# An RWKV-7 hybrid block on one Trainium2 core: the products of two heads on 64x64 quarters of the array

## The chip, the cores and the metric

The kernel runs on one core of one Trainium2 chip. The metric is the device time of one execution in microseconds (us), as the median of several runs; less is better. The engines are named as the profile names them: PE (TensorE matmul), PEld (TensorE weight load), DVE (VectorE), ACT (ScalarE), POOL (GpSimd) and SP (SyncE, which only issues DMAs here).

## The reference, cut to what matters

One decoder block over 512 tokens of width 2048: a normalised input is projected once, and an RWKV-7 time mixer of 16 heads of 64 and a sliding-window attention run on the result side by side. Gates merge them, and a gated ConvFFN follows. All data are float32. The change lies in the time mixer alone:

```python
def step(state, inp):
    r_t, k_t, v_t, w_t, ka_t, kb_t = inp
    sa = jnp.einsum('bhvk,bhk->bhv', state, ka_t)
    state = (state * w_t[:, :, None, :] + sa[..., None] * kb_t[:, :, None, :]
             + v_t[..., None] * k_t[:, :, None, :])
    y = jnp.einsum('bhvk,bhk->bhv', state, r_t)
    return state, y

state0 = jnp.zeros((B, RW_HEADS, RW_HEAD, RW_HEAD), f32)
_, y = lax.scan(step, state0, xs)
```

So each head has a 64x64 state, and the heads never meet inside the scan.

## The kernel before

The recurrence is computed in 8 chunks of 64 tokens (`NCH` = 8, `C` = 64), and the 16 heads in 8 pairs. A pair fills the 128 partitions: head 0 has the rows 0 to 63 and head 1 the rows 64 to 127 (`HV`). Because one matmul of the full 128x128 array serves both heads, the stationary operands are block diagonal: a 128x128 tile holds one head's 64x64 block in each of two corners and zeros in the others.

For a pair p the code runs `early(p)` (the projections of r, k and v, norms, decays), `late(p)` (the chunk products, the inverse, the chain over the chunks) and `final(p)` (the group norm and the gate). The order of emission is late(p), early(p+1), final(p), then three tiles of the gates' projections. The framework's planner lays out each engine's instructions anew from these, by its own costs, except where the code pins them (`pin`). The projections (`project`, L260 to L262, weights split by ACT in L243 and DVE in L244) are independent of the pairs, and the planner puts them between the matmuls of `late` while those wait for DVE or ACT.

In `late(p)`, with what the change touches:

- `BKK` (L672, L673) holds, for each chunk, the scaled `kb` of a head in the head's own half of the columns and its scaled `k2` in the other half. `BAR` (L674, L675) holds the scaled `kk` and `r`, block diagonal.
- L697 multiplies `BKK` with `BAR`, two chunks to a PSUM tile. L701 masks the result into four tiles: `BX` and `MD` (the kb parts, in the own block, mask "own") and `OA` and `MO` (the k parts, in the other head's block, mask "other"). L702 to L717 and the loop over `LEVELS` (L765 to L790) invert `BX` with f16 products, which the change leaves as they are.
- `VV` (L734) is v with its mean taken off, transposed. Since the k parts lie in the other half, head 0's v goes to the rows of head 1 and the reverse (`ol:oh`).
- `bulk_mm` (L718) runs one 128x128 matmul with 64 moving columns a chunk into one PSUM tile and copies it out with ACT: `GV` = OA x VV, and later `KV` = KO x VV, both through L721.
- `KD` and `KO` (L749, L750) come from transposes of `BKE` (L742): the kb blocks into `KD` in the diagonal corners, the k blocks into `KO` in the off corners. The other corners of `KO` are set to 0 by two POOL memsets (L745, L746) for each pair, as its buffer (tag "ko") serves `OA` and `yd` too.
- The chain over the chunks (L793 to L810): psG (L796, `BAR` x `SS`), added to `GV` by DVE (L798); psU (L802, `BX` x G), copied to `UU` by ACT (L803); psS (L809, `KD` x `UU`), added by DVE (L810) to make the next chunk's state `SS`.
- The output (L815, L816, L818) accumulates three products a chunk in one PSUM tile: `MO` x `VV`, `MD` x `UU`, `BAR` x `SS`.

That is 61 products of 128x128 weights with 64 moving columns for each pair: 8 + 8 (L721), 7 (psG), 8 (psU), 7 (psS), 8 + 8 + 7 (output).

Of the kernel before, what the change touches and what calls it, by code (L numbers as in the profile page):

```python
# [8 lines left out]
F32 = mybir.dt.float32  # L9
# [125 lines left out]
def block_kernel(ctx: ExitStack, tc: tile.TileContext, d: Dims, a: dict, out: bass.AP):  # L135
# [145 lines left out]
    if True:  # L281
# [243 lines left out]
        with ExitStack() as pr:  # L525
# [56 lines left out]
            MO, MD = (bd.tile([P, NCH, P], F32, name=n) for n in ("MO", "MD"))  # L582
# [9 lines left out]
            def r3(ap, c=C):  # L592
                return ap.rearrange("p (n c) -> p n c", c=c)
# [71 lines left out]
            def late(p, st):  # L665
# [27 lines left out]
                OA = wk.tile([P, NCH, P], F32, name="OA", tag="ko")  # L693
                for n0 in range(0, NCH, 2):
                    ps = bulk()
                    for j in range(2):
                        pe.matmul(ps[:, j * 4 * C : (j + 1) * 4 * C], BKK[:, n0 + j],  # L697
                                  BAR[:, n0 + j].rearrange("p a h c -> p (a h c)"), start=True, stop=True)
                    pq = ps.rearrange("p (n a c) -> p n a c", n=2, a=2)
                    for t, a, nm in ((BX, 0, "own"), (OA, 0, "other"), (MD, 1, "own"), (MO, 1, "other")):  # L700
                        dve.tensor_tensor(t[:, n0 : n0 + 2], pq[:, :, a], mb(nm, 2)[:, :, a * P : (a + 1) * P], op=ALU.mult)  # L701
                for g in range(2):  # L702
# [13 lines left out]
                    for i in range(2):  # L716
                        dve.tensor_tensor(BT[:, i, ns], AI[:, i, ns], mb("t1bd", HN), op=ALU.mult)  # L717
                def bulk_mm(dst, l, r):  # L718
                    ps = bulk()
                    for n in range(NCH):  # L720
                        pe.matmul(r3(ps)[:, n], l(n), r(n), start=True, stop=True)  # L721
                    act.activation(dst, r3(ps), AF.Copy)
# [8 lines left out]
                for a, (fl, fh) in enumerate(HV):  # L731
                    for h in range(2):
                        ol, oh = HV[1 - h]
                        dve.tensor_tensor(VV[ol:oh, a::2], r3(ps)[fl:fh, h::2],  # L734
                                          vm[fl:fh, h::2].unsqueeze(2).to_broadcast([C, NT, C]), op=ALU.add)
                GV = wk.tile([P, NCH, C], F32, name="GV", tag="yt")
                bulk_mm(GV, lambda n: OA[:, n], lambda n: VV[:, n])
                for g in range(2):
# [4 lines left out]
                    if g == 0:  # L743
                        KO = wk.tile([P, NCH, P], F32, name="KO", tag="ko")
                        pool.memset(KO[0:C, :, 0:C], 0.0)  # L745
                        pool.memset(KO[C:P, :, C:P], 0.0)  # L746
                    for h, (lo, hi) in enumerate(HV):
                        ol, oh = HV[1 - h]
                        act.activation(KD[lo:hi, ns, lo:hi], ps[lo:hi, :, lo:hi], AF.Copy)  # L749
                        act.activation(KO[lo:hi, ns, ol:oh], ps[lo:hi, :, ol:oh], AF.Copy)  # L750

# [41 lines left out]
                for n in range(NCH):  # L793
                    if n:
                        ps = chn.tile([P, C], F32, name="psG", tag="chn")
                        pe.matmul(ps, BAR[:, n, 0].rearrange("p h c -> p (h c)"), SS[:, n], start=True, stop=True)  # L796
# [5 lines left out]
                    pe.matmul(ps, BX[:, n], G, start=True, stop=True)  # L802
# [6 lines left out]
                    pe.matmul(ps, KD[:, n], UU[:, n], start=True, stop=True)  # L809
# [3 lines left out]
                for n in range(NCH):  # L813
                    dst = r3(ps)[:, n]
                    pe.matmul(dst, MO[:, n], VV[:, n], start=True, stop=False)  # L815
                    pe.matmul(dst, MD[:, n], UU[:, n], start=False, stop=n == 0)  # L816
                    if n:
                        pe.matmul(dst, BAR[:, n, 1].rearrange("p h c -> p (h c)"), SS[:, n], start=False, stop=True)  # L818
# [626 lines left out]
```

## Time and profile before

| what | us |
|---|---|
| median of 3 runs (2877.95 to 2883.97) | 2881.03 |
| the profiled execution's own time | 2880.39 |
| its span | 2878.6 |
| stage of the eight pairs, from the trace | about 330 to 1135 |

A program matmul in float32 shows as two records of PE (and two weight loads of PEld), one in float32r or f16, and a transpose, as one. A row of the timeline has the start, the length, the engine, the line, the operation, what it writes and reads, and how many records in a row it merges; "128*128" is rows by columns of the weights, and the shape behind it that of the moving operand. A record's length is that of its way through the array, so records overlap, and what a matmul costs is read from the distance between the starts. A row of a group has the count, the busy us, the mean ns of one, and the idle time of the engine just before.

### The profile page before, as it was taken

Reading aid. Unit: us, or ns where it says so; the run is one execution under the profiler, and the core shown is the slowest. Engines: PE = TensorE matmul, PEld = TensorE weight load, DVE = VectorE, ACT = ScalarE, POOL = GpSimd, SP = SyncE. Lnnn points to the kernel's source line nnn. Section 1 sums busy time; section 2 is a strip of 40 time slices with the busy share of each in tenths; the row PEclk is TensorE's granted clock in tenths of the full one; section 3 lists DMA queues with packets and bytes.
Section 4 is the critical chain, followed back from the end, with each engine's and each line's share of the span. In section 5 each row is a group of like instructions: output and inputs, shape, how many; then the busy total and the mean of one; then the engine's idle time right before and its main releaser. Section 6 shows DMA issues by size and latency. Waiting matters only on the chain.

```text
span 2878.6 us, 46868 instructions
## 1 busy us (share of the span) xinstructions
PE 2823.6 (98%) x17970; PEld 2476.8 (86%) x17970; DVE 1968.5 (68%) x3388; ACT 1319.8 (46%) x2190; POOL 235.8 (8%) x319
## 2 busy tenths in 40 slices
PE   7999999999999999999999899999999999999999
PEld 6888778878878878788888899999999999888887
DVE  5666677777776775345668787877777787665555
ACT  5345344334434434322456455455555545544444
POOL 0101000000000001011000001101011110000000
PEclk9999999999999999999999999999999999999999
DMA  6865666666656657878777788888888888877775
GB/s 196 227 161 148 184 161 166 155 166 153 165 144 162 169 154 187 269 234 277 255 261 207 211 229 226 224 239 241 227 226 231 239 238 220 316 244 243 257 255 190
DMA packets 223856, 608.35 MB, mean 211 GB/s; under 512 B 24576, under 2 KB 44688, under 8 KB 222608
## 3 DMA queue, kind: packets, MB, share of 16 engines
q1 hardware_dynamic: 156096, 432.86, 45.9%
q0 software_dynamic: 36832, 134.24, 24.3%
q10 hardware_dynamic: 30704, 38.27, 3.9%
q8 instruction: 141, 2.31, 0.3%
q14 instruction: 83, 0.68, 0.1%
HBM read 554.59 MB, written 174.40 MB: 253 GB/s over the span
## 4 chain that ended last, share of the span: by engine, by line
PE 87%; DVE 6%; DMA 3%; issue 1%; ACT 1%; ACTq 0%; SPq 0%; POOL 0%; DVEq 0%; POOLq 0%
PE X L1146 17%; PE X L1013 10%; PE acc L262 9%; PE acc L260 9%; PE acc L261 9%; PE Y L1013 9%; PE Y L1146 8%; PE Z L1146 4%; PE bulk L721 1%; PE bulk L788 1%; PE bulk L758 1%; PE mi L513 1%; PE bulk L606 1%; DMA raw<-in_w_dn_dram 1%; DVE BT L717 1%
## 5 line engine op out<-in xcount | busy, mean ns | idle before, releaser
L260 PE MATMUL acc<-xhi,whi 128*128 128x512 f32 x1120 | 454.1, 405 | 1.8 <-ACT whi L243 1.8
L261 PE MATMUL acc<-xlo,whi 128*128 128x512 f32 x1120 | 454.0, 405 | 0.0
L262 PE MATMUL acc<-xhi,wlo 128*128 128x512 f32 x1120 | 448.6, 401 | 3.2 <-DVE wlo L244 3.2
L243 ACT ACTIVATE whi<-raw 128x512 fp32r<-128x512 f32 x352 | 220.7, 630 | 468.8 <-PE acc L261 364.5
L244 DVE TENSOR_TENSOR wlo<-raw,whi 128x512 fp32r<-128x512 f32 x352 | 240.5, 689 | 231.5 <-ACT whi L243 206.9
L1006 DVE TENSOR_TENSOR wlo<-raw,whi 128x1024 fp32r<-128x1024 f32 x210 | 257.2, 1225 | 204.4 <-ACT whi L1005 204.3
L1005 ACT ACTIVATE whi<-raw 128x1024 fp32r<-128x1024 f32 x210 | 222.6, 1060 | 290.5 <-PE X L1013 155.1
L1146 PE MATMUL X<-b,whi 128*128 128x256 f32 x1472 | 271.0, 284 | 2.5 <-DVE u L1166 0.9
L1146 PE MATMUL X<-t,whi 128*128 128x256 f32 x1408 | 261.2, 286 | 10.1 <-DVE u L1166 9.6
L1129 DVE TENSOR_TENSOR wlo<-raw,whi 128x1024 fp32r<-128x1024 f32 x176 | 215.1, 1223 | 78.7 <-ACT whi L1128 78.3
L1146 PE MATMUL Y<-t,whi 128*128 128x256 f32 x1408 | 257.6, 283 | 0.0
L262 PEld LDWEIGHTS acc<-xhi,wlo 128*128 128x128 f32 x1120 | 212.0, 189 | 45.3 <-DVE wlo L244 7.0
L261 PEld LDWEIGHTS acc<-xlo,whi 128*128 128x128 f32 x1120 | 212.3, 190 | 38.4 <-issue 2.2
L260 PEld LDWEIGHTS acc<-xhi,whi 128*128 128x128 f32 x1120 | 211.8, 189 | 38.7 <-ACT whi L243 2.2
L1128 ACT ACTIVATE whi<-a 128x1024 fp32r<-128x1024 f32 x132 | 139.4, 1056 | 216.2 <-DVE a L1122 212.6
L1146 PEld LDWEIGHTS X<-b,whi 128*128 128x128 f32 x1472 | 231.1, 193 | 3.3 <-issue 2.4
L1146 PEld LDWEIGHTS X<-t,whi 128*128 128x128 f32 x1408 | 222.9, 195 | 10.7 <-DVE u L1166 7.1
L1146 PEld LDWEIGHTS Y<-t,whi 128*128 128x128 f32 x1408 | 220.2, 192 | 0.0
L1146 PE MATMUL X<-b,wlo 128*128 128x256 f32 x736 | 209.5, 285 | 2.1 <-DVE wlo L1129 2.1
L1129 DVE TENSOR_TENSOR wlo<-a,whi 128x1024 fp32r<-128x1024 f32 x132 | 161.7, 1225 | 69.3 <-ACT whi L1128 68.6
L1146 PE MATMUL X<-t,wlo 128*128 128x256 f32 x704 | 200.9, 285 | 0.0
L1146 PE MATMUL Y<-t,wlo 128*128 128x256 f32 x704 | 199.5, 283 | 0.0
(776 smaller groups left out, 6027.2 us busy)
## 6 DMA issues: line engine op xcount, KB each, us to landing
raw<-in_w_up_dram SPq DMA_DIRECT2D x180, 512.0 KB
raw<-in_w_z_dram SPq DMA_DIRECT2D x288, 256.0 KB
s_dn<-in_w_dn_dram POOLq DMA_DIRECT2D x88, 512.0 KB, 7.0
raw<-in_w_up_dram POOLq DMA_DIRECT2D x88, 512.0 KB, 8.6
raw<-s_dn SPq DMA_DIRECT2D x88, 512.0 KB
raw<-in_w_dn_dram SPq DMA_DIRECT2D x66, 512.0 KB
a<-in_w_up_dram SPq DMA_DIRECT2D x48, 512.0 KB
s_dn<-in_w_dn_dram SPq DMA_DIRECT2D x44, 512.0 KB
```

The lines of the kernel that those rows point to most:

```text
L243: pin(act.activation(hi, raw, AF.Copy))
L244: pin(dve.tensor_tensor(lo, raw, hi.bitcast(F32), op=ALU.subtract))
L260: pe.matmul(acc, whi[:, j], xhi[:, k], start=first, stop=False)
L261: pe.matmul(acc, whi[:, j], xlo[:, k], start=False, stop=False)
L262: pe.matmul(acc, wlo[:, j], xhi[:, k], start=False, stop=last)
L513: pe.matmul(ps[:, h], pT[:, kb, h], vt[:, n - 1 + kb, g * HD : (g + 1) * HD], start=kb == kbs[0], stop=kb == kbs[-1])
L1005: act.activation(whi, wr, AF.Copy)
L1006: dve.tensor_tensor(wlo, wr, whi.bitcast(F32), op=ALU.subtract)
L1013: pe.matmul(dst, l[:, q, ts], r[:, es], start=fst and j == 0, stop=lst and j == 2, skip_group_check=True)
L1128: pin(act.activation(hi, t, AF.Copy))
L1129: pin(dve.tensor_tensor(lo, t, hi.bitcast(F32), op=ALU.subtract))
L1146: pin(pe.matmul(ps, l[:, k], r[:, k], start=start and k + i == 0, stop=last and i == 2, skip_group_check=True))
```

## The change

All 61 products are made by head: `heads_mm` runs one matmul on the rows and columns 0 to 63 of the array, then one on 64 to 127, so each uses a 64x64 quarter on the diagonal and reads only its head's block. For that, each head's k parts move into its own rows: `AM` takes the place of `OA` and `MO`, 64 columns wide, written by DVE from the other half's rows of PSUM; `KO` becomes 64 columns wide, written by ACT across the halves, without its memsets; and `VV` stays in its head's own rows. The matmul of L697, the inverse and all transposes stay on the full array.

```diff
--- before.py
+++ after.py
@@ -579,7 +579,8 @@
             BAR = bd.tile([P, NCH, 2, 2, C], F32, name="BAR")
             pool.memset(BAR[0:C, :, :, 1], 0.0)
             pool.memset(BAR[C:P, :, :, 0], 0.0)
-            MO, MD = (bd.tile([P, NCH, P], F32, name=n) for n in ("MO", "MD"))
+            MD = bd.tile([P, NCH, P], F32, name="MD")
+            AM = bd.tile([P, NCH, 2, C], F32, name="AM")
             KD = bdtile("KD")
             SS, UU, VV, KV = (bd.tile([P, NCH, C], F32, name=n) for n in ("SS", "UU", "VV", "KV"))
             Et = bd.tile([P, NCH, C + 1], F32, name="Et")
@@ -690,15 +691,19 @@
 
                 BKE = wk.tile([P, NCH, P], F32, name="BKE", tag="BKE")
                 dve.tensor_tensor(BKE, BKK, ee.unsqueeze(2).to_broadcast([P, NCH, P]), op=ALU.mult)
-                OA = wk.tile([P, NCH, P], F32, name="OA", tag="ko")
                 for n0 in range(0, NCH, 2):
                     ps = bulk()
                     for j in range(2):
                         pe.matmul(ps[:, j * 4 * C : (j + 1) * 4 * C], BKK[:, n0 + j],
                                   BAR[:, n0 + j].rearrange("p a h c -> p (a h c)"), start=True, stop=True)
                     pq = ps.rearrange("p (n a c) -> p n a c", n=2, a=2)
-                    for t, a, nm in ((BX, 0, "own"), (OA, 0, "other"), (MD, 1, "own"), (MO, 1, "other")):
-                        dve.tensor_tensor(t[:, n0 : n0 + 2], pq[:, :, a], mb(nm, 2)[:, :, a * P : (a + 1) * P], op=ALU.mult)
+                    for t, a in ((BX, 0), (MD, 1)):
+                        dve.tensor_tensor(t[:, n0 : n0 + 2], pq[:, :, a], mb("own", 2)[:, :, a * P : (a + 1) * P], op=ALU.mult)
+                    for h, (lo, hi) in enumerate(HV):
+                        rs = slice(*HV[1 - h])
+                        mk = K["other"].rearrange("p (a c) -> p a c", a=2)[rs, :, lo:hi]
+                        dve.tensor_tensor(AM[lo:hi, n0 : n0 + 2], pq[rs, :, :, lo:hi],
+                                          mk.unsqueeze(1).to_broadcast([C, 2, 2, C]), op=ALU.mult)
                 for g in range(2):
                     ns = slice(g * HN, (g + 1) * HN)
                     for h, (lo, hi) in enumerate(HV):
@@ -715,10 +720,15 @@
                     dve.tensor_scalar(BX[C:P, ns, C:P], tt[C:P, ns], 1.0 / SG, None, op0=ALU.mult)
                     for i in range(2):
                         dve.tensor_tensor(BT[:, i, ns], AI[:, i, ns], mb("t1bd", HN), op=ALU.mult)
+                def heads_mm(dst, l, r, start, stop):
+                    for h, (lo, hi) in enumerate(HV):
+                        w = l[lo:hi] if l.shape[-1] == C else l[lo:hi, lo:hi]
+                        pe.matmul(dst[lo:hi], w, r[lo:hi], start=start, stop=stop, skip_group_check=True)
+
                 def bulk_mm(dst, l, r):
                     ps = bulk()
                     for n in range(NCH):
-                        pe.matmul(r3(ps)[:, n], l(n), r(n), start=True, stop=True)
+                        heads_mm(r3(ps)[:, n], l(n), r(n), True, True)
                     act.activation(dst, r3(ps), AF.Copy)
 
                 ps = bulk()
@@ -729,25 +739,22 @@
                 dve.reduce_sum(vm, r3(ps), axis=AX.X)
                 dve.tensor_scalar(vm, vm, -1.0 / HD, None, op0=ALU.mult)
                 for a, (fl, fh) in enumerate(HV):
-                    for h in range(2):
-                        ol, oh = HV[1 - h]
-                        dve.tensor_tensor(VV[ol:oh, a::2], r3(ps)[fl:fh, h::2],
+                    for h, (lo, hi) in enumerate(HV):
+                        dve.tensor_tensor(VV[lo:hi, a::2], r3(ps)[fl:fh, h::2],
                                           vm[fl:fh, h::2].unsqueeze(2).to_broadcast([C, NT, C]), op=ALU.add)
                 GV = wk.tile([P, NCH, C], F32, name="GV", tag="yt")
-                bulk_mm(GV, lambda n: OA[:, n], lambda n: VV[:, n])
+                bulk_mm(GV, lambda n: AM[:, n, 0], lambda n: VV[:, n])
                 for g in range(2):
                     ns = slice(g * HN, (g + 1) * HN)
                     ps = bulk().rearrange("p (n c) -> p n c", c=P)
                     for j in range(HN):
                         pe.transpose(ps[:, j], BKE[:, g * HN + j], ident)
                     if g == 0:
-                        KO = wk.tile([P, NCH, P], F32, name="KO", tag="ko")
-                        pool.memset(KO[0:C, :, 0:C], 0.0)
-                        pool.memset(KO[C:P, :, C:P], 0.0)
+                        KO = wk.tile([P, NCH, C], F32, name="KO", tag="ko")
                     for h, (lo, hi) in enumerate(HV):
                         ol, oh = HV[1 - h]
                         act.activation(KD[lo:hi, ns, lo:hi], ps[lo:hi, :, lo:hi], AF.Copy)
-                        act.activation(KO[lo:hi, ns, ol:oh], ps[lo:hi, :, ol:oh], AF.Copy)
+                        act.activation(KO[ol:oh, ns], ps[lo:hi, :, ol:oh], AF.Copy)
 
                 bulk_mm(KV, lambda n: KO[:, n], lambda n: VV[:, n])
 
@@ -793,29 +800,29 @@
                 for n in range(NCH):
                     if n:
                         ps = chn.tile([P, C], F32, name="psG", tag="chn")
-                        pe.matmul(ps, BAR[:, n, 0].rearrange("p h c -> p (h c)"), SS[:, n], start=True, stop=True)
+                        heads_mm(ps, BAR[:, n, 0].rearrange("p h c -> p (h c)"), SS[:, n], True, True)
                         G = wk.tile([P, C], F32, name="G", tag="G", bufs=2)
                         dve.tensor_tensor(G, GV[:, n], ps, op=ALU.add)
                     else:
                         G = GV[:, 0]
                     ps = chn.tile([P, C], F32, name="psU", tag="chn")
-                    pe.matmul(ps, BX[:, n], G, start=True, stop=True)
+                    heads_mm(ps, BX[:, n], G, True, True)
                     act.activation(UU[:, n], ps, AF.Copy)
                     if n == NCH - 1:
                         break
                     if n:
                         dve.scalar_tensor_tensor(KV[:, n], SS[:, n], ee[:, n : n + 1], KV[:, n], op0=ALU.mult, op1=ALU.add)
                     ps = chn.tile([P, C], F32, name="psS", tag="chn")
-                    pe.matmul(ps, KD[:, n], UU[:, n], start=True, stop=True)
+                    heads_mm(ps, KD[:, n], UU[:, n], True, True)
                     dve.tensor_tensor(SS[:, n + 1], KV[:, n], ps, op=ALU.add)
 
                 ps = bulk()
                 for n in range(NCH):
                     dst = r3(ps)[:, n]
-                    pe.matmul(dst, MO[:, n], VV[:, n], start=True, stop=False)
-                    pe.matmul(dst, MD[:, n], UU[:, n], start=False, stop=n == 0)
+                    heads_mm(dst, AM[:, n, 1], VV[:, n], True, False)
+                    heads_mm(dst, MD[:, n], UU[:, n], False, n == 0)
                     if n:
-                        pe.matmul(dst, BAR[:, n, 1].rearrange("p h c -> p (h c)"), SS[:, n], start=False, stop=True)
+                        heads_mm(dst, BAR[:, n, 1].rearrange("p h c -> p (h c)"), SS[:, n], False, True)
                 yt = wk.tile([P, NCH, C], F32, name="yt", tag="yt")
                 act.activation(yt, r3(ps), AF.Copy)
                 return ag, bon, yt
```

## What the change should do to the time, predicted before it ran

> **What bounds the kernel now.** I read the page first: the busy shares and the chain that ended last. Both name TensorE.
>
> ```profile
> PE 2823.6 (98%) x17970; PEld 2476.8 (86%) x17970; DVE 1968.5 (68%) x3388; ACT 1319.8 (46%) x2190; POOL 235.8 (8%) x319
> PE 87%; DVE 6%; DMA 3%; issue 1%; ACT 1%; ACTq 0%; SPq 0%; POOL 0%; DVEq 0%; POOLq 0%
> ```
>
> A busy matmul row is no proof by itself, since records overlap. So I asked for the stage that the change touches, from the first to the last pair of heads, by the view of windows (length, then busy us of PE, PEld, DVE, ACT, POOL).
>
> ```profile
> 330.00:1135.00 805.00, 795.92 (x5213) 644.38 (x5211) 573.04 (x1377) 343.30 (x748) 63.55 (x86) 1.00 0.63 159
> ```
>
> PE is busy 796 of 805 us at full clock, DVE 573, ACT 343, the DMA engines 63%. The stage holds eight pairs, some 100 us each. What counts is how far apart the matmuls start, which the timeline of PE shows.
>
> ```profile
> 355.99 1.08 PE L721 MATMUL bulk<-VV,KO 128*128 128x64 f32 x8
> 356.90 0.19 PE L758 MATMUL bulk<-XIW,AI 128*128 128x64 f16 x1
> 356.93 0.18 PE L759 MATMUL bulk<-XIW,AI 128*128 128x32 f16 x1
> ...
> 359.04 0.40 PE L260 MATMUL acc<-xhi,whi 128*128 128x512 f32 x1
> ...
> 361.32 0.39 PE L261 MATMUL acc<-xlo,whi 128*128 128x512 f32 x1
> ```
>
> Between 359.04 and 361.32 lie ten projection matmuls, 0.228 us each. The eight records of L721 take 0.91 us, 0.114 each (the other places round to 0.112, which I use). One program matmul in float32 makes two records, so a 128x64 product costs 0.224 us, as much as a projection with eight times the columns. Why 0.112? Look at a record whose weights were already there:
>
> ```profile
> 402.80 0.33 PE L796 MATMUL psG<-SS,BAR 128*128 128x64 f32 x2
> ...
> 403.25 0.40 PE L261 MATMUL acc<-xlo,whi 128*128 128x512 f32 x1
> 403.49 0.39 PE L802 MATMUL psU<-G,BX 128*128 128x64 f32 x2
> 403.69 0.48 PE L262 MATMUL acc<-xhi,wlo 128*128 128x512 f32 x1
> 404.01 0.40 PE L260 MATMUL acc<-xhi,whi 128*128 128x512 f32 x1
> 404.24 0.39 PE L809 MATMUL psS<-UU,KD 128*128 128x64 f32 x2
> 404.46 0.39 PE L816 MATMUL bulk<-UU,MD 128*128 128x64 f32 x2
> 404.69 0.39 PE L818 MATMUL bulk<-SS,BAR 128*128 128x64 f32 x2
> 404.91 0.39 PE L815 MATMUL bulk<-VV,MO 128*128 128x64 f32 x2
> 405.11 0.48 PE L261 MATMUL acc<-xlo,whi 128*128 128x512 f32 x1
> 405.42 0.39 PE L262 MATMUL acc<-xhi,wlo 128*128 128x512 f32 x1
> 405.65 0.33 PE L796 MATMUL psG<-SS,BAR 128*128 128x64 f32 x2
> ...
> L796 PE MATMUL psG<-SS,BAR x112: 217/248/275, 396.2 to 1128.8; 128*128 128x64 f32 x112
> ```
>
> Two psG records together last 0.33, one lasts up to 0.275: the second started 0.055 after the first. So 64 columns stream in 0.055, and the other 0.057 of a usual record is its weight load of 128 columns. These products are bound by weight loads, and half of what is loaded is zeros: the other head's block.
>
> **The change part by part.** How many products? The groups by form, over the stage:
>
> ```profile
> L815 PE MATMUL bulk<-VV,MO 128*128 128x64 f32 x128 | 25.0, 277 | 0.0
> L816 PE MATMUL bulk<-UU,MD 128*128 128x64 f32 x128 | 24.3, 271 | 0.0
> ...
> L818 PE MATMUL bulk<-SS,BAR 128*128 128x64 f32 x112 | 21.6, 275 | 0.0
> L809 PE MATMUL psS<-UU,KD 128*128 128x64 f32 x112 | 21.2, 271 | 0.0
> L802 PE MATMUL psU<-G,BX 128*128 128x64 f32 x112 | 21.0, 270 | 0.6 <-DVE G L798 0.6
> L796 PE MATMUL psG<-SS,BAR 128*128 128x64 f32 x112 | 18.5, 246 | 0.0
> L721 PE MATMUL bulk<-VV,KO 128*128 128x64 f32 x128 | 17.2, 278 | 0.4
> L721 PE MATMUL bulk<-VV,OA 128*128 128x64 f32 x128 | 16.1, 269 | 0.0
> ...
> L802 PE MATMUL psU<-GV,BX 128*128 128x64 f32 x16 | 2.6, 247 | 0.0
> ```
>
> These are 976 records, 488 products, 61 a pair; at 0.112 they hold 109 us of PE. Each becomes two program matmuls of 64x64, four records A1 A2 B1 B2. With half the columns a load takes 0.056, about the 0.055 that a stream takes. No row shows a matmul on fewer than 128 rows, so the price of a pair of heads has two ends. If B's quarter works fully beside A's, it is A's two passes alone: 2 x 0.056 = 0.112. If they go one after the other, 4 x 0.056 = 0.224, what it costs today. In between, B may start a little after A2, and the next A after B2; about the smallest step between two starts in the stage is 0.03 (356.90 to 356.93, L758 to L759). With one such step a product is 0.135 or so, with two 0.166. I take **0.135**: the nearest row is the one that shows load and stream of different matmuls side by side (0.112 for work that one after the other would be 0.167), so the array does run pieces together that don't touch the same weights. It is a choice, not a measurement.
>
> A stretch also pays at its end: the next projection's 128 columns load only after the last pass has begun, 0.112. So a stretch of n products costs (n-1) x 0.135 + 0.139 + 0.112. By stretches, counted in the timeline of 330 to 1135 us, of which the rows above show one chunk of the chain:
>
> - Lone psG and psU between projections, 99: today psU costs 404.01 - 403.25 less two projections, 0.30; after, 0.25. They gain next to nothing; I take 0.
> - psS with the three output products, 48: today 405.42 - 404.01 less two projections, 0.95; after 0.656. 48 x 0.30 = 14 us.
> - L721: a pair has two stretches of four (KO) and one of seven or eight (OA). 16 x (0.91 - 0.57) + 8 x 0.45 = 9 us. The rest, some tens of single products beside other float32 work, 1 us.
>
> That is 24 us of the 109. KO's two memsets go too:
>
> ```profile
> L745 POOL MEMSET KO<- x8: 517/519/519, 354.4 to 1074.0; 64x512 f32 x8
> ...
>   PE bulk L721: 115.1, 7
> ...
>   POOL KO L746: 3.7, 8
> ```
>
> PE's weight loads waited 3.7 us for them in all, partly under a running stream: 0 to 3.7, I take 2. The memset itself stood 115 us in POOL's queue ahead of the adding DMAs of the later stages (L228); these issue earlier, nothing in this stage reads them, so 0 either way. No DMA is added or moved, and no wait: KO's copies still wait for the same transposes, OA's place is taken by AM, which waits like MO for the last output products of the pair before.
>
> On DVE, the masked products of OA and MO become two of 64 rows with as many elements a row:
>
> ```profile
> L701 DVE TENSOR_TENSOR OA<-bulk,cst 128x256 f32<-128x256 f32 x32 | 13.4, 418 | 0.0
> ...
> L734 DVE TENSOR_TENSOR VV<-bulk,vm 64x256 f32<-64x256 f32 x32 | 13.5, 423 | 0.7
> ```
>
> 64 of 0.418 go and 64 of 0.423 (the row that also crosses halves) come: +0.3 us, under PE, as DVE has 232 us free. VV's and KO's copies keep size and number. Without that cover it would be 0.3 us.
>
> Sum: 24 + 2 = 26 us off the profiled execution, which took 2880.39 us (span 2878.6 and 1.8 around it; 0.6 below the median 2881.03): **2854**. With overlap at its best (0.112) the stretches give 36 and the memsets 4, so 2840; with two steps (0.166) 17 and 0, so 2863. [...]
>
> **Changing the shape of the array.** The stretches are entered and left 26 times a pair, 416 changes in all. The trace has one matmul with fewer columns than 128, the transpose of L377:
>
> ```profile
> 396.89 0.39 PE L802 MATMUL psU<-G,BX 128*128 128x64 f32 x2
> 397.01 0.14 PEld L377 LDWEIGHTS bulk<-ident,rq 128*8 128x8 f32 x1
> 397.12 0.27 PE L377 MATMUL bulk<-ident,rq 128*8 128x128 f32 x1
> ...
> 397.23 0.59 PE L628 MATMUL bulk<-thw,wl 128*128 128x512 f32 x1
> ```
>
> psU's two records take 0.23 and L377 0.11 before the next full matmul starts: its stream and nothing more. A load of 8 columns is shorter, too. I cost a change at 0. [...]
>
> **The rivals.** *The heads don't overlap.* All four passes go one after the other at 0.056. For it: no row shows overlap of quarters, and both heads write one PSUM tile. Against: loads and streams do overlap. Lone products gain 0.02, the fours stay at 0.95 (15 x 0.056 + 0.112), so the sum is 0 to -2: 2878 to 2882. [...]
>
> *Changing rows drains the array.* Price: a record of 0.275 has 0.163 left when the next usually starts (0.112 on). With 416 changes that is 68 us, against 26 gained: 2922. It turns slower from 26/416 = 0.063 a change on. For it: no row with fewer rows. Against: L377.
>
> *The chain becomes the bound.* A chunk takes 405.65 - 402.80 = 2.85 us. psG to psU and psU to psS are 0.69 and 0.75 apart, and the two that a DVE or ACT step must fit between lie only two projections apart. The chunk would shrink by 0.3, out of psS to psG (1.41), so the close links stay. If the planned order of PE, which is laid out anew, fits worse, PE idles 0.1 to 0.2 at some of the 22 links a pair: 10 to 26 us given back, 2864 to 2880.
>
> *It doesn't do what it says:* the planner puts projections between A and B. Then lone stretches double and each costs its 0.112: as the first rival or some us worse.
>
> **How the numbers follow.** Forecast with its own range (2840 to 2863): 0.5. Chain gives part back, still faster by over 0.2% (5.8 us, about what a measurement of this kernel can tell): 0.1. No overlap, or all given back, within 0.2%: 0.19. Drains, or doubled stretches: 0.21. The range must reach the no-overlap case and half of the drains (0.1 a change, +15 us): 2838 to 2896. Faster 0.6, same 0.19, slower 0.21.
>
> **What would show it.** In the profile after: records of 64*64; in a stretch of psS and output products, starts of one head's pair 0.056 apart and a product each 0.11 to 0.17 (0.22: no overlap); a projection after a stretch starting no later than today (later by 0.1 or more: drain); lone psG unchanged; KO's memsets gone and OA's products not waiting. The forecast is wrong if product times stay at 0.22, if gaps stand at the borders, or if PE's idle time before psU, psS and psG grows.

## The result, and the profile after

The changed kernel takes 2918.57 us (median of 4 runs, 2915.94 to 2921.25), the kernel before 2880.15 (4 runs, 2877.95 to 2883.97). The ratio is 1.014, with a 95% interval of 1.0122 to 1.0157: 38 us slower. The forecast was 2854, with a range of 2838 to 2896, so both the direction and the range were wrong. A ratio leaves out an execution at a far lower mean clock (one of 3935 us at 0.65 in the first of the kernels with psU alone below, one of 3076 us at 0.85 in the second), while a median counts it.

The profiled execution took 2915.94 us, with a span of 2914.1, 35.5 more than before. The page first, with the same two lines as before:

```profile
PE 2851.2 (98%) x18946; PEld 2443.1 (84%) x18946; DVE 1973.7 (68%) x3388; ACT 1320.3 (45%) x2190; POOL 227.0 (8%) x303
PE 86%; DVE 7%; DMA 3%; ACT 1%; issue 1%; ACTq 0%; SPq 0%; DVEq 0%; POOLq 0%
```

PE has 976 more records, as it should, and is still the bound. DVE's share of the chain has grown from 6 to 7%. All the loss must lie in the pairs' stage. A good ruler for it is the tile `VV`, which DVE writes once a pair: its first and last start lie seven pairs apart. From the view of that tile, before and after (count, ns, first and last start):

```profile
L734 DVE TENSOR_TENSOR VV<-bulk,vm x32: 417/422/429, 350.7 to 1071.5; 64x256 f32<-64x256 f32 x32
```

```profile
L743 DVE TENSOR_TENSOR VV<-bulk,vm x32: 409/422/428, 352.4 to 1111.3; 64x256 f32<-64x256 f32 x32
```

Seven pairs took 720.8 us and take 758.9: **38.1 us**, all of the 35.5 between the two profiled executions and 2.6 more. Every kernel below is read by this ruler, because it leaves out the start, the end and the rest of the program. It is one execution of each, and whole executions of the kernel before differ by up to 6 us.

**What did the products do?** The timeline of PE, one chunk of the chain (four records make one product; the prediction shows the same chunk of before):

```profile
402.94 0.39 PE L260 MATMUL acc<-xhi,whi 128*128 128x512 f32 x1
403.26 0.33 PE L726 MATMUL psU<-G,BX 64*64 64x64 f32 x4
403.53 0.50 PE L261 MATMUL acc<-xlo,whi 128*128 128x512 f32 x1
403.86 0.40 PE L262 MATMUL acc<-xhi,wlo 128*128 128x512 f32 x1
404.19 0.33 PE L726 MATMUL psS<-UU,KD 64*64 64x64 f32 x4
404.36 0.28 PE L726 MATMUL bulk<-UU,MD 64*64 64x64 f32 x4
404.47 0.28 PE L726 MATMUL bulk<-SS,BAR 64*64 64x64 f32 x4
404.59 0.28 PE L726 MATMUL bulk<-VV,AM 64*64 64x64 f32 x4
404.80 0.50 PE L260 MATMUL acc<-xhi,whi 128*128 128x512 f32 x1
405.23 0.33 PE L726 MATMUL psG<-SS,BAR 64*64 64x64 f32 x4
```

Two things stand here. Inside a stretch the products start 404.36 to 404.47 to 404.59, **0.115 us apart**, where the full array needed 0.224: the two heads do run side by side. But every border is late. From the start of a projection to the first product lie 0.32 to 0.33 us (402.94 to 403.26, 403.86 to 404.19), where two projections follow each other at 0.228. The first product of a stretch lasts 0.17 instead of 0.115 (404.19 to 404.36), the last one 0.21 (404.59 to 404.80). The lone psU now costs 403.86 - 402.94 less two projections, 0.46; before it was 0.30.

The weight loads show the border from the other side (timeline of PEld, before and after, at the same psU):

```profile
403.44 0.30 PEld L802 LDWEIGHTS psU<-G,BX 128*128 128x128 f32 x2 [0.23 <-DVE G L798]
...
403.77 0.19 PEld L260 LDWEIGHTS acc<-xhi,whi 128*128 128x128 f32 x1
```

```profile
403.26 0.19 PEld L726 LDWEIGHTS psU<-G,BX 64*64 64x64 f32 x4 [0.37 <-issue]
403.52 0.19 PEld L261 LDWEIGHTS acc<-xlo,whi 128*128 128x128 f32 x1
403.63 0.19 PEld L262 LDWEIGHTS acc<-xhi,wlo 128*128 128x128 f32 x1
```

Before, psU's load began at 403.44, 0.05 ahead of its stream, while a projection ran, and L260's at 403.77, 0.24 ahead of its own. After, the loads of both sides of a border begin with their streams (403.26, and 403.52 for L261 at 403.53); the load unit had stood 0.37 us for nothing that the profile shows. Only L262's load, with no border ahead of it, still comes 0.23 early (403.63 for 403.86). It is the same at the other borders of the seven pairs: loads begin 0.002 us ahead of their streams (the median of 201 entries into a stretch and of 200 exits), against 0.224 between two projections. So in these seven pairs weights aren't loaded ahead across a change of the array's shape.

**What did DVE do?** PE's waits in the stage name it. The view of waits (in total, times, longest), before and after:

```profile
PE acc L262 <- DVE wlo L244: 3.2, 8, 1.2
```

```profile
PE acc L262 <- DVE wlo L244: 10.0, 8, 1.3
```

PE waits 0.85 us longer in each pair for `wlo`, a split of projection weights. The timeline of DVE in the masked products shows why (before, then after; first op, a part, and the op that follows the section):

```profile
437.90 0.42 DVE L701 TENSOR_TENSOR BX<-bulk,cst 128x256 f32<-128x256 f32 x1
438.24 0.42 DVE L701 TENSOR_TENSOR OA<-bulk,cst 128x256 f32<-128x256 f32 x1
...
443.20 0.85 DVE L705 TENSOR_TENSOR tt<-BX,cst 64x256 f32<-64x256 f32 x2
```

```profile
442.61 0.42 DVE L701 TENSOR_TENSOR BX<-bulk,cst 128x256 f32<-128x256 f32 x1
442.95 0.41 DVE L701 TENSOR_TENSOR MD<-bulk,cst 128x256 f32<-128x256 f32 x1
443.38 0.86 DVE L705 TENSOR_TENSOR AM<-bulk,cst 64x256 f32<-64x256 f32 x2
444.26 0.42 DVE L701 TENSOR_TENSOR BX<-bulk,cst 128x256 f32<-128x256 f32 x1
...
449.25 0.85 DVE L710 TENSOR_TENSOR tt<-BX,cst 64x256 f32<-64x256 f32 x2
```

The records are as long as before (0.42), but length isn't the price. Two operations of 128 rows start 0.33 apart, the second before the first has ended. The two of 64 rows take 0.88 from start to start (443.38 to 444.26), 0.44 each, and the `MD` ahead of them takes 0.43 (442.95 to 443.38). The 16 operations took 443.20 - 437.90 = 5.30 us and take 449.25 - 442.61 = 6.64: **1.34 us more a pair**.

**And the clock.** The view of windows has the granted clock (the third number from the right):

```profile
568.60:575.40 6.80, 6.80 (x78) 5.24 (x80) 2.81 (x7) 4.27 (x11) 0.81 (x1) 0.50 0.76 233
677.80:684.60 6.80, 6.80 (x69) 5.24 (x69) 2.97 (x6) 3.95 (x10) 0.81 (x1) 0.50 0.84 247
1002.10:1008.90 6.80, 6.80 (x72) 4.99 (x73) 2.69 (x6) 4.52 (x11) 0.81 (x1) 0.50 0.82 254
```

In three of the seven pairs PE runs at half clock for 6.8 us, soon after its wait for `wlo`; the timeline of PE has the first of these waits:

```profile
566.33 0.50 PE L262 MATMUL acc<-xhi,wlo 128*128 128x512 f32 x1 [1.25 <-DVE wlo L244]
```

The slow stretch begins 2.3 us later, at 568.6, and there are three of them: 3 x 6.8 / 2 = 10.2 us, an estimate from the granted clock of 0.50. Before has no such stretch in its seven pairs (1.00). The records of PE show the loss too: from L262, over 42 records of products, four of L751 and 16 in f16, to the next L260, it took 5.17 us from 568.84 on, and 3.05 for the same records in the pair of 461.83, at full clock; by that share the three cost 8.4. The longest wait for `wlo` was 1.3 us; what sets the drop off was not settled.

So there are three suspects: borders, DVE's 64-row operations, and the clock. A first theory held all three; its rival was that borders alone, or something else in the quarters, made the loss.

### The profile page after: what moved, and what is told of

The parts are those of the page before. It is cut to its first block, busy times and chain, and to the rows that moved or that the text cites. A ratio compares the mean times of both kernels' runs of the same rounds, so it can differ in the third digit from the quotient of the medians.

```text
span 2914.1 us, 48752 instructions
## 1 busy us (share of the span) xinstructions
PE 2851.2 (98%) x18946; PEld 2443.1 (84%) x18946; DVE 1973.7 (68%) x3388; ACT 1320.3 (45%) x2190; POOL 227.0 (8%) x303
## 3 DMA queue, kind: packets, MB, share of 16 engines
q1 hardware_dynamic: 156096, 432.86, 46.5%
## 4 chain that ended last, share of the span: by engine, by line
PE 86%; DVE 7%; DMA 3%; ACT 1%; issue 1%; ACTq 0%; SPq 0%; DVEq 0%; POOLq 0%
PE X L1153 17%; PE X L1020 11%; PE acc L262 9%; PE acc L261 9%; PE acc L260 9%; PE Y L1020 8%; PE Y L1153 8%; PE Z L1153 4%; PE bulk L726 2%; PE bulk L795 1%; PE bulk L765 1%; PE mi L513 1%; DVE AM L705 1%; DVE wlo L244 1%; PE bulk L607 1%
## 5 line engine op out<-in xcount | busy, mean ns | idle before, releaser
L262 PE MATMUL acc<-xhi,wlo 128*128 128x512 f32 x1120 | 449.9, 402 | 10.0 <-DVE wlo L244 10.0
L260 PE MATMUL acc<-xhi,whi 128*128 128x512 f32 x1120 | 456.8, 408 | 2.0 <-ACT whi L243 2.0
L261 PE MATMUL acc<-xlo,whi 128*128 128x512 f32 x1120 | 453.2, 405 | 0.0
L262 PEld LDWEIGHTS acc<-xhi,wlo 128*128 128x128 f32 x1120 | 211.3, 189 | 53.7 <-DVE wlo L244 14.1
L260 PEld LDWEIGHTS acc<-xhi,whi 128*128 128x128 f32 x1120 | 211.4, 189 | 46.0 <-ACT whi L243 2.4
L261 PEld LDWEIGHTS acc<-xlo,whi 128*128 128x128 f32 x1120 | 211.2, 189 | 42.3 <-issue 1.9
```

The lines of the kernel that those rows point to most:

```text
L260: pe.matmul(acc, whi[:, j], xhi[:, k], start=first, stop=False)
L261: pe.matmul(acc, whi[:, j], xlo[:, k], start=False, stop=False)
L262: pe.matmul(acc, wlo[:, j], xhi[:, k], start=False, stop=last)
```

## Experiments

Each is read by the ruler as "seven pairs against before": the last start of `VV` less the first, against 720.8. On the full array a product is 0.224 and on quarters 0.115, so I count 0.109 gained for each.

### The border by itself: psU alone

Three kernels change only psU of the kernel before, 64 of them with a full-array product or projection on each side. The first puts them on quarters:

```diff
-                    pe.matmul(ps, BX[:, n], G, start=True, stop=True)
+                    for lo, hi in HV:
+                        pe.matmul(ps[lo:hi], BX[lo:hi, n, lo:hi], G[lo:hi], start=True, stop=True, skip_group_check=True)
```

> The kernel before, with only the chain's psU (64 products, nearly all alone between full-array matmuls) on two 64x64 quarters; no data moved. Theory 1 (borders: each stretch on quarters costs the array some 0.34 us more at its two ends than on the full array, against 0.109 us gained per product): 64 x (0.34 - 0.11) = +15 us, about 2895. Theory 2 (the moved data and the planner's new order cost the time, the quarters themselves gain): 64 x -0.11 = -7 to 0 us, 2873 to 2880.

The second keeps 128 rows and halves the columns (`BX[:, n, lo:hi], G`):

> The kernel before, with only psU split by columns: two matmuls of 128 rows and 64 columns each, the rows of the other head being zeros. Theory 1a (any change of the array's shape costs, columns as rows): about +15 us, as with quarters. Theory 1b (only a change of rows costs; the transpose with 8 columns showed nothing): between -7 and +1 us, starts at the borders as in the kernel before. Theory 2: as 1b.

The third keeps 128 columns and halves the rows, and leaves out head 1's part of U (`BX[0:C, n], G[0:C]`):

> The kernel before, with psU made of one matmul of 64 rows and 128 columns, head 0's rows alone; head 1's part of U is left out (it becomes zero). A product costs what it did (two records of 128 columns, 0.112 us each), so only the border is left. Theory 1a and 1b: 64 x 0.2 to 0.34 = +13 to +22 us, about 2897. If only narrowed columns cost: 0 us.

Measured: 2890.35 (ratio 1.0029, 1.0011 to 1.0047), 2887.13 (1.0024, 1.0014 to 1.0034) and 2895.91 (1.0058, 1.0041 to 1.0075). The view of the tile `VV` in the first, the second and the third:

```profile
L734 DVE TENSOR_TENSOR VV<-bulk,vm x32: 416/422/429, 353.5 to 1081.9; 64x256 f32<-64x256 f32 x32
```
```profile
L734 DVE TENSOR_TENSOR VV<-bulk,vm x32: 416/422/428, 352.3 to 1080.7; 64x256 f32<-64x256 f32 x32
```
```profile
L734 DVE TENSOR_TENSOR VV<-bulk,vm x32: 416/422/428, 349.2 to 1082.4; 64x256 f32<-64x256 f32 x32
```

Seven pairs take 7.6 us more in the first, as much in the second, and 12.4 in the third, for 56 stretches. In the third, nothing is gained (two records of 128 columns, as before), so 12.4 / 56 = **0.22 us is the bare border, in and out**; it may be more, as the other three executions took 8 us longer than the profiled one. In the first, 7.6 / 56 = 0.14 is left after a gain of 0.109: a border of 0.245. Narrowing the columns alone costs the same as narrowing both, if its product gains as much. So the two changes of a stretch cost 0.22 to 0.25 us in the first and the third. The prediction had costed a change at 0 from the transpose of L377, 128 rows by 8 columns. In the first of these kernels L377 follows psU directly:

```profile
399.92 0.33 PE L803 MATMUL psU<-G,BX 64*64 64x64 f32 x4
400.19 0.27 PE L377 MATMUL bulk<-ident,rq 128*8 128x128 f32 x1
400.30 1.02 PE L628 MATMUL bulk<-thw,wl 128*128 128x512 f32 x2
```

From quarters into L377 is a border (0.27, as into the projection at 403.53 above), and from L377 to the full matmul behind it is none (0.11). Why 8 columns of 128 pass as a full array and 64 don't isn't known.

### The data moved, the products on the full array

The changed kernel with `AM` as two block-diagonal tiles and `heads_mm` as one matmul:

```diff
-                    for h, (lo, hi) in enumerate(HV):
-                        w = l[lo:hi] if l.shape[-1] == C else l[lo:hi, lo:hi]
-                        pe.matmul(dst[lo:hi], w, r[lo:hi], start=start, stop=stop, skip_group_check=True)
+                    pe.matmul(dst, l, r, start=start, stop=stop, skip_group_check=True)
```

> The changed kernel's data in the own head's rows, but every product on the full array: AM as two block diagonal tiles with zero corners, KO written into the first of them, yd in another buffer. DVE has 128 masked products of 64x128 for 64 of 64x256, some 5 us more under PE. Theory 1: as the kernel before, 2875 to 2886. Theory 2 (the move of the data and what the planner makes of it is the loss): 2895 to 2918.

Measured: 2909.33 (1.0108, 1.0093 to 1.0123). This run was meant to isolate the data's part and doesn't: PE stood waiting for `VV`, and that came with seven stretches at half clock, 22 us lost by the trace's record of the clock. By the ruler it takes 34.9 us more. The waits of PE in it:

```profile
PE bulk L725 <- DVE VV L742: 21.0, 7, 3.4
```

That wait isn't in the changed kernel. What the run shows is only how dear a late DVE is here.

### The quarters without the data moved

The kernel before, its data and DVE operations as they were, with GV, KV, psG, psU and psS on quarters (the off-diagonal ones for GV and KV), output products on the full array:

```diff
+                def heads_mm(dst, l, r, other=False):
+                    for h, (lo, hi) in enumerate(HV):
+                        rl, rh = HV[1 - h] if other else (lo, hi)
+                        pe.matmul(dst[lo:hi], l[rl:rh, lo:hi], r[rl:rh], start=True, stop=True, skip_group_check=True)
...
-                        pe.matmul(ps, BAR[:, n, 0].rearrange("p h c -> p (h c)"), SS[:, n], start=True, stop=True)
+                        heads_mm(ps, BAR[:, n, 0].rearrange("p h c -> p (h c)"), SS[:, n])
```

> The kernel before, its data where they were; psG, psU, psS and the GV and KV products on quarters (the k blocks on the two off-diagonal quarters), the output products on the full array. 304 products in 224 stretches. Theory 1 (a stretch costs 0.29 us at its two ends, a product gains 0.109): 65 - 33 = +32 us, about 2911. Theory 2 (the moved data and the plan are the loss, as the run of the layout on the full array suggests): 2846 to 2880.

Measured: 2914.48 (1.0117, 1.0102 to 1.0132), as theory 1 has it. Its `VV`:

```profile
L739 DVE TENSOR_TENSOR VV<-bulk,vm x32: 416/422/428, 350.2 to 1104.0; 64x256 f32<-64x256 f32 x32
```

Seven pairs take 753.8, 33.0 more, with no half-clock stretch and `wlo` waiting 3.2 us as before. Its 266 products in seven pairs gain 29.0, so 196 stretches cost 62, **0.316 each**. That is more than a lone psU showed. A part of it may be what the changed kernel's timeline shows above: a single projection with stretches on both sides pays on entry and exit (404.80 to psG at 405.23 is 0.43 us).

### Longer stretches

Three kernels go from the changed one towards fewer borders. First, psG, psU and psS back on the full array (139 stretches instead of 228). Second, the output products also held in one run behind the last psU (56):

```diff
-                    heads_mm(dst, AM[:, n, 1], VV[:, n], True, False)
-                    heads_mm(dst, MD[:, n], UU[:, n], False, n == 0)
+                    heads_mm(dst, AM[:, n, 1], VV[:, n], True, False, True)
+                    heads_mm(dst, MD[:, n], UU[:, n], False, n == 0, True)
...
```

The last argument pins these matmuls in program order.

Third, GV's products also emitted behind the transposes of `BKE`, in one run with KV's (40):

```diff
-                bulk_mm(GV, lambda n: AM[:, n, 0], lambda n: VV[:, n])
                 for g in range(2):
...
+                bulk_mm(GV, lambda n: AM[:, n, 0], lambda n: VV[:, n])
                 bulk_mm(KV, lambda n: KO[:, n], lambda n: VV[:, n])
```

> The changed kernel with psG, psU and psS back on the full array: 312 products on quarters in 139 stretches. Theory 1: 40 - 34 = +6 us against before, about 2886, and 32 less than the change. Theory 2: the data are still moved, so 2900 to 2918.

> As the run before, and the output products held in program order behind the last psU of the pair, so that they make one stretch: 312 products in 56 stretches. Theory 1: 16 - 34 = -18 us, about 2862. Theory 2: 2900 to 2918.

> As the run before, and GV's products emitted behind the transposes of BKE, in one run with KV's: 312 products in 40 stretches. Theory 1: 12 - 34 = -22 us, about 2857. Theory 2: 2900 to 2918.

Measured: 2897.95 (1.0062, 1.0047 to 1.0077), 2891.62 (1.0045, 1.0029 to 1.0062) and **2867.81 (0.9964, 0.9951 to 0.9977)**. By the ruler they take 19.3 and 14.6 us more than before and 5.5 less. The order is as expected, the sizes aren't: all are 10 us or more above. In the first, PE still waits 9.9 us for `wlo`, and 5.1 us go at half rate. The waits of PE in the second and the third show what stood there:

```profile
PE acc L262 <- DVE wlo L244: 9.9, 8, 1.2
PE bulk L660 <- DVE lw L658: 6.7, 7, 1.0
```

```profile
PE bulk L660 <- DVE lw L658: 6.6, 7, 1.0
PE bulk L726 <- DVE VV L745: 2.5, 7, 0.4
...
PE acc L262 <- DVE wlo L244: 0.5, 1, 0.5
```

In the second, `wlo` waits as in the changed kernel, and the record of the clock has 15 us of the seven pairs lost at half rate; in the third that wait is gone, with GV's run at another place in PE's order, and so are the half-clock stretches in the stage. Both pay a new wait: with the outputs at the end of a pair, the next pair's L660 comes before DVE has its `lw`. With fewer stretches and no late `wlo`, quarters win.

### DVE by itself

The kernel before, all on the full array, with MO's masked product as two operations of 64 rows in two of the four groups:

```diff
-                        dve.tensor_tensor(t[:, n0 : n0 + 2], pq[:, :, a], mb(nm, 2)[:, :, a * P : (a + 1) * P], op=ALU.mult)
+                        for lo, hi in HV if t is MO and n0 % 4 else ((0, P),):
+                            dve.tensor_tensor(t[lo:hi, n0 : n0 + 2], pq[lo:hi, :, a],
+                                              mb(nm, 2)[lo:hi, :, a * P : (a + 1) * P], op=ALU.mult)
```

> The kernel before, every product on the full array; only MO's masked product is written as two operations of 64 rows instead of one of 128 for half of its groups, 16 more DVE operations a pair by way of 0.33 to 0.44 us, minus what a pair of groups saved, no PE instruction added. Theory 1 (the mask section of a pair is bound by DVE, and a late DVE there is paid twice, as PE's wait and as the clock that follows it): some 1 us a pair of PE waiting for wlo or for the masked data, and clock drops like those of the changed kernel: +8 to +20 us, 2888 to 2900. Theory 2 (DVE's time lies under PE, all of the loss of the changed kernel is borders): no change, 2880 within 0.2%.

Measured: 2889.72 (1.0043, 1.0028 to 1.0058), against 2876.39 for the kernel before on that chip. The expectation's count is wrong: it is 16 operations more in the whole program, two a pair. Timeline of DVE, and the tile `VV`:

```profile
441.49 0.42 DVE L702 TENSOR_TENSOR BX<-bulk,cst 128x256 f32<-128x256 f32 x1
...
443.48 0.41 DVE L702 TENSOR_TENSOR MD<-bulk,cst 128x256 f32<-128x256 f32 x1
443.81 0.85 DVE L702 TENSOR_TENSOR MO<-bulk,cst 64x256 f32<-64x256 f32 x2
...
447.90 0.86 DVE L707 TENSOR_TENSOR tt<-BX,cst 64x256 f32<-64x256 f32 x2
```

```profile
L736 DVE TENSOR_TENSOR VV<-bulk,vm x32: 416/422/428, 353.4 to 1082.1; 64x256 f32<-64x256 f32 x32
```

The section takes 447.90 - 441.49 = 6.41 us, 1.11 more than before, and seven pairs take 728.7, 7.9 more: 1.13 a pair. In this section **what DVE's work gains in length, the kernel loses, one for one**. No half clock lies in its seven pairs, although PE waits 9.7 us for `wlo`, about as long as in the changed kernel. The two operations read and write the same rows, so no crossing of the halves is needed for a loss.

But it isn't the 64 rows as such either. The first half of `MO` starts 0.33 after `MD` (443.48 to 443.81), as an operation of 128 rows does; both begin at row 0. The kernel with the data moved and the products on the full array has four operations of 64 rows in a row, two for each half, with records of 0.27 to 0.29:

```profile
442.92 1.00 DVE L706 TENSOR_TENSOR AM<-bulk,cst 64x128 f32<-64x128 f32 x4
```

They take 1.03 us to the start of the next `BX` (443.95): in each of the trace's 32 such groups the two of one half start 0.21 apart, so they overlap, and the next operation starts 0.30 after the second of them. What fits all these distances is a change of the first row: an operation that reads or writes from other rows than the one ahead starts when that one has ended. In the changed kernel `MD` to `AM` (which reads from row 64), `AM` to `AM` and `AM` to `BX` take 0.43, 0.44 and 0.45 in place of 0.33, which makes 0.33 a group and the 1.3 a pair. No kernel was run that only orders the operations by half.

### The changed kernel with one operation for AM

```diff
-                    for h, (lo, hi) in enumerate(HV):
-                        rs = slice(*HV[1 - h])
...
+                    dve.tensor_tensor(AM[:, n0 : n0 + 2], pq[:, :, :, 0:C],
+                                      mk.unsqueeze(1).to_broadcast([P, 2, 2, C]), op=ALU.mult)
```

> The changed kernel with AM written by one operation of 128 rows a group, with no crossing of halves: DVE has 3 operations a group instead of 4, PE's instructions keep kind and number. Left out: the crossing, so that the own head's rows of AM hold the other half's columns. Theory 1 (38 us of loss are borders plus 10 to 20 us of DVE's waits and clock): the waits for wlo go back to 3 us, the clock drops go, 2896 to 2903. Theory 2 (borders alone): 2918, as the changed kernel.

Measured: 2887.39 (1.0038, 1.0023 to 1.0053), 29 us less than the changed kernel by the two ratios (1.0% of 2880). Timeline of DVE, and the tile `VV`:

```profile
440.97 0.42 DVE L701 TENSOR_TENSOR BX<-bulk,cst 128x256 f32<-128x256 f32 x1
...
444.95 0.84 DVE L708 TENSOR_TENSOR tt<-BX,cst 64x256 f32<-64x256 f32 x2
```

```profile
L741 DVE TENSOR_TENSOR VV<-bulk,vm x32: 407/423/428, 350.3 to 1084.3; 64x256 f32<-64x256 f32 x32
```

Seven pairs take 734.0, 24.9 less than in the changed kernel, with the same quarters. Its clock is full there (1.00 granted), which is 10.2 of the 24.9; the other 14.7 go with 6.64 - 3.98 = 2.66 us less of DVE's section a pair, 18.6 in seven, most of which comes through. So borders alone can't be it: they hardly differ (228 stretches there, 226 here). The run lies below the band expected; the expectation had forgotten that its section is shorter than even that of the kernel before (3.98 against 5.30), which may be the reason.

### Quarters in place, in few stretches

The kernel before with GV, KV and two of three output products on quarters, the outputs behind the chain (56 stretches). All MO products are issued ahead of the others into the same PSUM tile, and a part of the output is lost; what PE runs is as named.

```diff
+                    pin(pe.matmul(r3(ps)[:, n], MO[:, n], VV[:, n], start=True, stop=False, skip_group_check=True))
...
-                    pe.matmul(dst, MD[:, n], UU[:, n], start=False, stop=n == 0)
+                    heads_mm(dst, MD[:, n], UU[:, n], False, n == 0)
```

> The kernel before with its data and DVE operations as they were; on quarters only GV, KV (off the diagonal) and two of the three output products (MD and BAR), the outputs held behind the last psU of a pair, so that the quarter products stand in 56 stretches. Theory 1 (a product on quarters gains 0.11 us, a stretch costs 0.23 to 0.29): 248 x 0.109 = 27 less 56 x 0.29 = 16, 11 us faster, 2869 (2867 to 2874), and no wait of DVE added. Theory 2 (quarters are slower for another reason than the number of stretches): 2880 or more, with the share of in_place, 248 of 304 products, +28: 2908.

Measured: 2875.05 against 2876.39 (1.0, 0.9988 to 1.0011): neither. The waits of PE tell where the 11 us stayed:

```profile
PE bulk L659 <- DVE lw L657: 9.1, 7, 1.3
```

It is the wait for `lw` that the held outputs bring, 9.1 us, and not more work for DVE. By the ruler the kernel takes 1.7 us more: 217 products gain 23.7, 49 stretches at 0.316 cost 15.5, and with the wait that makes 0.9 more. A price that grows with the products (9 over 248) would look the same in the time, so one more kernel was needed.

### Only the bulk products, in runs of eight

The kernel before with GV and KV alone on quarters, nothing else moved. The products that need the last rows of `VV` or `KO` come first, so the planner has no reason to put anything between:

```diff
-                def bulk_mm(dst, l, r):
+                def bulk_mm(dst, l, r, rows=HV):
...
-                    for n in range(NCH):
-                        pe.matmul(r3(ps)[:, n], l(n), r(n), start=True, stop=True)
+                    for n in reversed(range(NCH)):
+                        for (rl, rh), (lo, hi) in zip(rows, rows[::-1]):
+                            mm = pe.matmul(r3(ps)[lo:hi, n], l(n)[rl:rh, lo:hi], r(n)[rl:rh], start=True, stop=True)
+                            if n < NCH - 1 or (rl, rh) != rows[0]:
+                                pin(mm)
...
-                bulk_mm(KV, lambda n: KO[:, n], lambda n: VV[:, n])
+                bulk_mm(KV, lambda n: KO[:, n], lambda n: VV[:, n], HV[::-1])
```

> The kernel before with its data, its chain and its output products on the full array; only GV and KV on quarters, off the diagonal, each of the eight chunks' products in one stretch, the products that need the last rows of VV or KO first, so that nothing comes between: 16 stretches of 8 products, 128 products in all, no DVE operation added, no output product moved. Theory 1 (a product on quarters gains 0.109 us, a stretch costs 0.23 to 0.29, DVE's time and moved outputs made the rest of the losses): 128 x 0.109 = 14 less 16 x 0.29 = 5, 9 us faster than the kernel before (7 to 11, ratio 0.997), and no wait for lw of more than 1 us. Theory 2 (the 9 us that the kernel with two of three output products on quarters fell short of are a price of the quarters that grows with the number of products, 9 / 248 = 0.036 each): 5 us less, 4 us faster or nothing.

Measured: **2865.48 (0.9952, 0.9938 to 0.9966)**: 14 us faster than before (10 to 18), at the upper end of theory 1 or beyond, and against theory 2. Timeline of PE, and the tile `VV`:

```profile
356.48 0.40 PE L262 MATMUL acc<-xhi,wlo 128*128 128x512 f32 x1
356.84 1.15 PE L722 MATMUL bulk<-VV,OA 64*64 64x64 f32 x32
357.92 1.09 PE L745 MATMUL bulk<-ident,BKE 128*128 128x128 f32 x8
```

```profile
L737 DVE TENSOR_TENSOR VV<-bulk,vm x32: 415/422/428, 355.0 to 1067.0; 64x256 f32<-64x256 f32 x32
```

Eight products and their borders take 357.92 - 356.48 less a projection's 0.228, 1.21 us; on the full array they took 8 x 0.224 = 1.79. Seven pairs take 712.0, 8.8 less, as theory 1 has it (112 x 0.109 less 14 stretches of 0.24). That the median gained some 5 more than the profiled run isn't explained. No wait for `lw` is in its list. It is faster than both the kernel before and the changed one.

## Why the prediction was wrong

**The bound and the overlap were right.** PE sets the time, the products were bound by weight loads, and two quarters run side by side. A product takes 0.115, better than the 0.135 that I took. "The heads don't overlap" is refuted. The prediction took the load of 128 columns once as 0.057, behind a stream, and once as 0.112; with two loads of 64 columns a head in 0.115, the second fits. Over seven pairs 427 products gain 427 x 0.109 = 46.5 us.

**The step that failed is "I cost a change at 0".** It rested on L377 alone. Measured, a stretch costs 0.22 bare (psU on 64 rows) to 0.316 (quarters in place). The changed kernel has 228 stretches, so in seven pairs 199.5 x 0.316 = 63 us. Of the rivals, "changing rows drains the array" came true in its price, with 0.11 to 0.16 a change for its 0.163, and its 2922 is 3 us off. That closeness is partly luck: its sum had 26 gained and 68 lost on borders, and nothing for DVE or the clock. Narrowing columns costs as much as rows, so it isn't the rows. Whether the array drains there, no run shows.

The number to work out was products per stretch. One gains 0.109 and a stretch costs 0.316, so a stretch pays from three products on. The change has 488 in 228 stretches, 2.1 each.

**The second step that failed is "+0.3 us, under PE, as DVE has 232 us free".** I priced operations by the length of their records, and by the share of DVE over the stage. Start to start, an operation took 0.33 before; three in each group of four, those around a change of rows, take 0.43 to 0.45 now, so the section grew by 1.34 us a pair. And it has no cover there: seven pairs at 1.13 / 1.11 of that give 9.6 us.

**The third term I didn't have at all**: half clock, 10.2 us in the profiled run by the granted clock. Why it fell on three pairs stays open.

Together over seven pairs: -46.5 + 63.0 + 9.6 + 10.2 = 36.3 of the 38.1 measured. The prices of the borders and of DVE come from other kernels (quarters in place, DVE by itself), so the sum is no fit to the changed kernel. The prices aren't sharp, though: with 0.245 a stretch it would be 22. Put to the three kernels with longer stretches, with their waits for `lw` and `VV` and their half clock added, and DVE's 9.6 where `wlo` is late, the same prices give 23 and 17 us more and 10 less, for 19.3, 14.6 and 5.5 measured. So they hold to some 4 us.

**The smaller steps.** "Lone psG and psU gain next to nothing" expected 0.25 for a psU; it took 0.46, so they lose 0.16. The rival that the planner splits the heads came true in part: 38 of the 228 stretches hold one head. "The chain becomes the bound" didn't: PE waits for `SS` 1.3 us in all. The memsets' 2 us can't be seen in it.

**The range** reached to half of the drains, though a rival with a worked price stood at 2922 and nothing in the trace showed a change of rows.

## What to carry to other kernels

Count the borders first: what packing the array saves is per product (here 0.109 us), what it costs is per stretch (0.22 to 0.32), so batch packed products into long runs before splitting any, and leave lone ones alone. Price an operation by the distance between starts in its own surroundings, not by its record (on DVE, mind where the first row changes: here starts 0.42 to 0.46 us apart for 0.33), and look for its cover in the section where it runs, not in the engine's share of the stage. When an experiment moves work to make runs longer, look for the consumer that it now stands in front of: here L660 behind the held outputs took back 6 to 9 us.

## What was not expected of the hardware

- A stretch on part of the array costs 0.22 to 0.32 us in and out, whether it has half the rows, half the columns or both, and in the changed kernel weights are loaded 0.002 us ahead over the border, against 0.224 between two projections. A transpose with 8 columns shows no such border to the full array (0.11 from its start to the next). That difference stays open.
- DVE operations with records of 0.42 start 0.33 apart when they begin at the same row, and 0.42 to 0.46 apart when the first row changes. This is read from the distances in four kernels; no run changed it alone.
- PE ran at half clock for 6.8 us in three of the changed kernel's seven pairs. Every pair has the wait for `wlo`; the kernel with two more 64-row operations waits 9.7 us for it in all, against 10.0, and has no such stretch. So the wait may be needed, but it isn't enough. The traces give a hint: the record of the clock changes on a grid of 3.41 us (before and after, every stretch between two changes lasts a whole multiple of 3.413 us, 3.413 to 10.24 at half clock), and in the changed kernel only 3 projections start in each of the three grid windows just before half clock, against 4 to 10 in those that hold the other five waits (5 to 11 in the kernel with two more 64-row operations). It is no rule yet: that last kernel also has a window with one projection, at 353.8 us, and full clock behind it, and so has the changed kernel, at 503.7.
